# A two-layer decoder trunk on one core: branch B's units reordered, with scores two units ahead, and the sums for T1 to T4 read back from DRAM

## The chip, the cores and the metric

The kernel runs on one core of one Trainium2 chip. The metric is the device time of one execution in microseconds (us). The engines are named as in the profile: PE (TensorE, matmuls; PEld are its weight loads), DVE (VectorE), ACT (ScalarE), POOL (GpSimd) and SP (SyncE, which here only issues DMAs). L12 is line 12 of the kernel before.

## What is computed

Two layers, on x of 1024 tokens by 1024 channels, all in float32:

```python
h = rms_norm(x, g_pre)
p = h @ w_in          # 1024 x 7936: inputs of three branches, their gates, three merge gates
y_a = chunk_gmlp(u_a, v_a, ...) * silu(gate_a)            # per chunk of 128 tokens
y_b = sliding_window_attention(rope(q_b), rope(k_b), v_b, sinks) * silu(gate_b)
y_c = stick_breaking_attention(q_c, k_c, v_c) * silu(gate_c)
merged = sum(sigmoid(merge_gate_i + b_i) * (y_i @ w_branch_i) for i in "abc")
x = x + rms_norm(merged @ w_out, g_post)
```

Branch B has 8 query heads and 2 key heads of 64, in blocks of 128 queries that see 256 keys. Branch C has 4 heads of 128 and is causal over the whole sequence. Branch A normalises v_a per token and mixes the tokens of a chunk with a lower triangular matrix.

## The kernel before

**Precision.** PE multiplies in a format with fewer bits than float32. Every operand is therefore kept as two tiles, hi (a cast on ACT, L111) and lo (the rest, a subtraction on DVE, L112); `split` makes both. `mm3` (L127 to L130) adds up three matmuls: hi by hi, hi by lo, lo by hi. The transposed normalised input h stands in SBUF as such pairs, `h[hf]`, where hf is a half of 512 tokens.

**Tiles.** `new()` takes one of 27 slots of 128 x 1024 floats from the head of a queue, `done()` puts it back at the end. Which slot a tile gets, and so whose last reader it has to wait for, follows from the order of the program's text. PSUM has three kinds of buffers of two each: `pj`, `z` (1024 wide) and `ta`, which `ptr` (transposes) and `pav` (attention outputs) share.

**Order.** PE's order is the order of the text (`manual_schedule`). The order on ACT, DVE, POOL and SP is made by a planner at compile time from modelled durations; where two instructions are ready it takes the earlier one of the text, or the one under `high_priority`. At run time each engine and SP work strictly in that order, so an instruction that waits holds up all that follows on its engine. `tc.issue_after(ins)` puts the instructions of its block that run on the engine of `ins` behind `ins` in that engine's order.

**The stream.** The projections h @ w_in that the branches need are jobs in one queue (`queue_layer`). `proj_t` gives 16 tokens of three matmuls of 512 columns, `proj_n` 64 tokens of three of 256 columns. `fill(us)` runs tokens until their nominal values, 0.64 and 0.32, add up to us; `need(label)` runs tokens until a job is finished. `fill` puts PE work between the dependent steps of branches C and B while ACT, DVE and POOL prepare the next step. A job's weights are loaded and split when the job before it begins.

The order of jobs is: v0, q0, k0, q1, k1, v1, q2, k2, q3, k3 (branch C), kb, vb, qb0, ga0, ga1, qb1, qb2, qb3 (branch B and two gates of A), va0, va1, ua0 to ua3 (branch A).

When kb or a qb ends, `rope` (L278 to L292) rotates it: four DMAs on SP swap rows into a scratch tile, two products run on POOL (L289, L290), a sum on DVE (L291), then hi and lo on ACT and DVE (L303, L305 for keys; L342, L343 for queries).

**A layer's stages.** `first_h` (layer 0) or `project_out` of the layer before make h: `norm_a` squares, and scales a block of 128 tokens; `norm_b` transposes it on PE and splits it into h. Then come `branch_c`, `branch_b`, `dense`, `merges` and `project_out`.

- `branch_b` runs 8 units v, for a pair of heads hp = v // 2 and a half of the tokens. `scores(v)` makes 16 matmuls (L487), then evicts, masks and normalises on ACT, DVE and POOL. `transp` transposes the weights on PE (L520), splits them, and masks on POOL (L527). `attend` multiplies with v (L544) and evicts with ACT (L554) and DVE (L555). Here scores run one unit ahead. `FB` holds the fills: the first before the loop, then five per unit: before the attend of the unit before, before transp 0, before transp 1 (with `FB_MORE`), before attend(v,0), and after it.
- `Combine` prepares T1, T2, T4 and T3: sums and differences of quarters of h, right operands of a Strassen-like scheme with seven products. `total` (L679) adds hi and lo on POOL to get a quarter of h back. `go(spare)` takes as many of its six steps as there are slots free; it is called in units 6 and 7, and twice in `dense`.
- `dense` runs what is left of the stream, then 17 pairs of column blocks, each with the seven products B11, B21, T2, T3, T1, T4, B22 of 12 matmuls. Its pieces of branch A (`branch_a`, a generator, `next(a)`) begin with statistics and normalising of v_a on DVE (L614 to L620).
- `merges` multiplies gated branch outputs with w_branch, block by block; DVE gates the product (L930), POOL adds it (L935), and for the third branch a deferred `parts` splits the sum for `project_out`. A block half is 512 tokens of one `dm` (128 output channels): 12 matmuls.

Of the kernel before, what the change touches and what calls it, by code (L numbers as in the profile page):

```python
# [15 lines left out]
F32 = mybir.dt.float32  # L16
# [6 lines left out]
P = 128  # L23
# [12 lines left out]
FC = (0.6, 0.6, 1.2, 0.6)  # L36
FB = (4, 1.9, 1.9, 2.2, 2.8, 2.8)
FB_MORE = {1: 2.3, 2: 1.3}
# [3 lines left out]
def trunk(ctx, tc, x, w_in, gm_w_s, gm_b_s, gm_g, sinks, w_ba, w_bb, w_bc, b_merge, w_out,  # L42
# [187 lines left out]

    def norm_b(n, xn):

        hf, c = n // 4, (n % 4) * P
        pt = pz().rearrange("p (a b) -> p a b", a=KD)
        for k in range(KD):
            nc.tensor.transpose(pt[:, k], xn[:, k * P:(k + 1) * P], ident)
        split(h[hf][0][:, :, c:c + P], h[hf][1][:, :, c:c + P], pt)
        done(xn)


    def queue_layer(l, S):
# [111 lines left out]

        vcj(0); qk(0); qk(1); vcj(1); qk(2); qk(3)
        raw("kb", O_KB, 1.0, after_k)
        raw("vb", O_VB, 1.0, after_v)
        for hp in range(4):
            raw(("qb", hp), O_QB + hp * P, 0.125, lambda hp=hp: after_q(hp))
            if hp == 0:
                gate("a", 0)  # L360
                gate("a", 1)

        def ua(c):
# [4 lines left out]
            proj_t(f"ua{c}", l, O_UA + c * P, ev)  # L368
        va(0); va(1); ua(0); ua(1); ua(2); ua(3)

# [101 lines left out]
    def branch_b(l, S):  # L472
# [58 lines left out]
        def attend(v, q, p, o):  # L531
            hp, nh = divmod(v, 2)
            grp = hp // 2
            pc, pp, c, pv = p
            av = pav().rearrange("p (n e k) -> p n e k", n=2, e=2)

            def vs(nm, b):
                return S[nm][b // 4][:, ((b % 4) * 2 + grp) * P:((b % 4) * 2 + grp + 1) * P]
            for j in range(2):
                n = nh * 4 + q * 2 + j  # L540

                ops = [(vs("vd", n), t) for t in c] + ([(vs("dv", n), t) for t in pv] if n else [])
                for i, (w, t) in enumerate(ops):
                    nc.tensor.matmul(av[:, j], w, t.rearrange("p (e j) k -> p e j k", j=2)[:, :, j],  # L544
                                     start=i == 0, stop=i == len(ops) - 1)
            done(pc, pp)
            n = nh * 4 + q * 2
            tt = new()
            tmp = tt[:, :256].rearrange("p (n k) -> p n k", n=2)
            for e in range(2):  # L550

                a, b = slice(e * 64, e * 64 + 64), slice(64 - e * 64, 128 - e * 64)
                with tc.high_priority():
                    nc.scalar.copy(tmp[a], av[b, :, e])  # L554
                    nc.vector.tensor_tensor(o[a, n * P:(n + 2) * P].rearrange("p (n k) -> p n k", n=2), av[a, :, e],  # L555
                                            tmp[a], op=ALU.add)
            done(tt)
            if nh and q:
                nc.sync.dma_start(S["ob"][hp * P:(hp + 1) * P, :], o)
                done(o)  # L560

        need("ga0")
        fill(5)
        ready = {0: scores(0)}
        fill(FB[0])
        pend = None
        for v in range(8):
            if v % 2 == 0:
# [12 lines left out]
            fill(FB[2])  # L581
            s = ready.pop(v)
            p0 = transp(s, 0)
            fill(FB[3] + FB_MORE.get(v, 0))
            p1 = transp(s, 1)
            done(s)
            if v >= 6:
                S["T"].go(6)
            fill(FB[4])
            attend(v, 0, p0, o)  # L590
            fill(FB[5])
            pend = (v, 1, p1, o)
            if v == 7:
                S["T"].go(5)
        attend(*pend)
# [61 lines left out]
    class Combine:  # L657

        def __init__(self):
# [16 lines left out]
        def steps(self):  # L676
            def total(hf, k0, eng):
                r = new()
                eng.tensor_tensor(r.rearrange("p (k t) -> p k t", k=2), h[hf][0][:, k0:k0 + 2].bitcast(F32),  # L679
                                  h[hf][1][:, k0:k0 + 2].bitcast(F32), op=ALU.add)  # L680
                return r
# [5 lines left out]
            for kp in range(2):  # L687
                k0 = kp * 2
                r12, r11 = total(1, k0, nc.gpsimd), total(0, k0, nc.gpsimd)
                nc.vector.tensor_tensor(r11, r12, r11, op=ALU.subtract)  # L690
                keep("T1", r11)
                yield
                r22 = total(1, k0 + 4, nc.gpsimd)
                nc.vector.tensor_tensor(r12, r22, r12, op=ALU.subtract)
# [4 lines left out]
                yield  # L699
                r21 = total(0, k0 + 4, nc.gpsimd)  # L700
                nc.vector.tensor_tensor(r21, r21, r22, op=ALU.subtract)
# [15 lines left out]
    def dense(l, S):  # L717
# [165 lines left out]
    def merges(l, S):  # L883
# [25 lines left out]
        for i, (bi, br, dm) in enumerate(blocks):  # L909
# [11 lines left out]
            for hf in range(2):  # L921
# [4 lines left out]
                with tc.high_priority():  # L926
                    if bi == 0:
                        nc.vector.tensor_tensor(acc[dm][:, ts], sg[:, ts], z, op=ALU.mult)
                    else:
                        nc.vector.tensor_tensor(sg[:, ts], sg[:, ts], z, op=ALU.mult)  # L930
                if late:
                    late.pop()()
                if bi:
# [26 lines left out]
    def project_out(l, mg):  # L960
# [29 lines left out]
        for n in range(NB):  # L990
# [18 lines left out]
            if 2 <= n < 6:  # L1009
                norm_b(n - 2, xn.pop(n - 2))  # L1010
        for t in mg:
# [4 lines left out]
        done(gpre)  # L1016
        norm_b(4, xn.pop(4))
        tokens(2)
        norm_b(5, xn.pop(5))
        tokens(1)  # L1020
        norm_b(6, xn.pop(6))
        tokens(1)
        norm_b(7, xn.pop(7))
        tokens(4)
        return last

    def first_h():
# [11 lines left out]
        for n in range(NB + 2):  # L1039
            if n < NB:  # L1040
                xn[n], last = norm_a(xt[n], gpre)
            if 1 <= n <= NB:
                norm_b(n - 1, xn.pop(n - 1))
            if n >= 2:
                tokens(1)
# [23 lines left out]
    for l in range(L):  # L1069
        states.append({nm: dr.tile([512, T], F32, name=f"{nm}{l}") for nm in ("ga", "gb", "gc", "oa", "ob", "oc",  # L1070
                                                                                "ya", "yb", "yc")})
        states[l]["sg"] = dr.tile([3 * D, T], F32, name=f"sg{l}")

# [4 lines left out]
    with tc.manual_schedule(engines={mybir.EngineType.PE}):  # L1078
# [3 lines left out]
        for l in range(L):  # L1082
# [4 lines left out]
            need("k0")  # L1087
            S["T"] = Combine()
            branch_c(l, S)
# [43 lines left out]
```

## Time and profile before

| what | value |
|---|---|
| time, median of 3 runs | 2100.52 us (2100.18 to 2101.63) |
| time of the profiled execution | 2101.78 us |
| its span | 2100.1 us |
| mean granted clock of PE | 0.988 |
| DMA | 245.03 MB, mean 117 GB/s |

The profile's page gives the busy time of each engine within the span. Matmuls overlap, so PE's busy time contains no gaps between matmuls that follow each other, and its idle time is what waits leave. The granted clock is the share of full speed that PE was allowed; 1.00 is full. A row of waits reads "engine tile line <- who ended the wait: total us, times, longest". A row of a group reads "line engine operation out<-in shapes xcount | busy us, mean ns of one | idle before". A timeline row gives start and duration in us, and in brackets the idle time before it.

### The profile page before, as it was taken

The page shows a single profiled execution, that of the slowest core. Times are in us where ns is not written, and L with a number is a line of the kernel's source. Part 1 is how long each engine was busy: PE and PEld are TensorE (multiplying, and loading weights), DVE is VectorE, ACT ScalarE, POOL GpSimd, SP SyncE. Part 2 cuts the span into 40 slices and gives each one's busy share as a digit, 9 for nine tenths or more (in the row PEclk, how much of TensorE's full clock was granted, in tenths as well). Part 3 has the DMA queues.
Part 4 walks back from the last instruction along what each step waited for, and adds up shares of the span by engine and source line. Part 5 has one row for each costly group of instructions (what it writes and reads, how often), then busy time and mean ns, then how long its engine had stood idle before and what let it go on. Part 6 is the DMA issues. An engine that isn't in the chain of part 4 may idle for free. (4 is left out here: it accounts for less than half of the span.)

```text
span 2100.1 us, 26497 instructions
## 1 busy us (share of the span) xinstructions
PE 2015.5 (96%) x10193; PEld 1685.4 (80%) x10193; DVE 1222.6 (58%) x1601; ACT 801.4 (38%) x1471; POOL 539.1 (26%) x517
## 2 busy tenths in 40 slices
PE   8999897999999999999999998899899999999998
PEld 7898786977888888887898887689778888888876
DVE  5555644777676555644546566457667765555433
ACT  5444444543243334212334345444433443332121
POOL 0222313344333220240003122233533223103400
PEclk9999998999999999999999999999999999999999
DMA  4111222112766427632321111311147662376213
GB/s 161 34 47 32 70 71 65 37 50 81 266 235 231 140 87 264 221 110 81 111 71 31 49 53 41 91 51 51 41 141 253 237 220 94 120 254 216 81 50 130
DMA packets 148062, 245.03 MB, mean 117 GB/s; under 512 B 8104, under 2 KB 105440, under 8 KB 147936
## 3 DMA queue, kind: packets, MB, share of 16 engines
q1 hardware_dynamic: 141024, 218.17, 31.7%
q10 hardware_dynamic: 6912, 25.17, 3.0%
q8 instruction: 80, 1.31, 0.3%
q14 instruction: 46, 0.38, 0.1%
HBM read 166.76 MB, written 71.30 MB: 113 GB/s over the span
## 5 line engine op out<-in xcount | busy, mean ns | idle before, releaser
L128 PE MATMUL pj<-h,whi 128*128 128x512 f32 x700 | 286.3, 409 | 0.0
L129 PE MATMUL pj<-h,whi 128*128 128x512 f32 x700 | 278.3, 398 | 0.0
L130 PE MATMUL pj<-h,wlo 128*128 128x512 f32 x700 | 278.1, 397 | 0.0
L130 PEld LDWEIGHTS pj<-h,wlo 128*128 128x128 f32 x700 | 132.4, 189 | 31.8
L128 PEld LDWEIGHTS pj<-h,whi 128*128 128x128 f32 x700 | 133.2, 190 | 24.9
L129 PEld LDWEIGHTS pj<-h,whi 128*128 128x128 f32 x700 | 133.2, 190 | 23.5
L128 PE MATMUL pj<-whi,h 128*128 128x256 f32 x512 | 148.3, 290 | 0.0
L130 PE MATMUL pj<-whi,h 128*128 128x256 f32 x512 | 144.0, 281 | 0.9 <-DVE h L112 0.9
L129 PE MATMUL pj<-wlo,h 128*128 128x256 f32 x512 | 143.7, 281 | 0.0
L112 DVE TENSOR_TENSOR wlo<-wr,whi 128x1024 fp32r<-128x1024 f32 x80 | 104.9, 1314 | 65.4 <-ACT whi L111 65.4
L935 POOL TENSOR_TENSOR s<-s,s 128x512 f32<-128x512 f32 x56 | 78.6, 1407 | 240.5 <-DVE s L930 128.8
L111 ACT CAST whi<-wr 128x1024 fp32r<-128x1024 f32 x80 | 84.0, 1050 | 145.7 <-PE pj L129 94.4
L111 ACT CAST wop<-s 128x512 fp32r<-128x512 f32 x118 | 73.0, 620 | 171.1 <-PE pz L130 58.2
L112 DVE TENSOR_TENSOR wop<-wr,wop 128x512 fp32r<-128x512 f32 x120 | 103.6, 867 | 42.7 <-ACT wop L111 42.5
L111 ACT CAST wop<-wr 128x512 fp32r<-128x512 f32 x120 | 73.9, 619 | 140.3 <-PE ptr L130 31.3
L397 DVE TENSOR_TENSOR_SCAN s<-s,ones 128x128 f32<-128x128 f32 (+3 forms) x64 | 91.9, 1437 | 60.0 <-POOL s L392 59.7
L112 DVE TENSOR_TENSOR s<-ptr,s 128x512 fp32r<-128x512 f32 (+2 forms) x132 | 77.3, 589 | 67.3 <-ACT s L111 66.6
L112 DVE TENSOR_TENSOR wop<-s,wop 128x512 fp32r<-128x512 f32 x118 | 104.8, 888 | 18.2 <-ACT wop L111 17.9
L111 ACT CAST s<-s 128x512 fp32r<-128x512 f32 (+2 forms) x64 | 47.9, 751 | 171.2 <-POOL s L935 70.1
L128 PE MATMUL pj<-h,s 128*128 128x512 f32 x256 | 103.4, 404 | 5.8 <-ACT s L111 5.8
L130 PE MATMUL pj<-h,s 128*128 128x512 f32 x256 | 102.8, 402 | 1.8 <-DVE s L112 1.8
L129 PE MATMUL pj<-h,s 128*128 128x512 f32 x256 | 102.9, 402 | 0.0
(231 smaller groups left out, 5231.0 us busy)
## 6 DMA issues: line engine op xcount, KB each, us to landing
wr<-in_w_in_dram SPq DMA_DIRECT2D x96, 512.0 KB, 3.9
sg<-s ACTq DMA_DIRECT2D x48, 512.0 KB, 4.9
s<-sg SPq DMA_DIRECT2D x48, 512.0 KB, 5.5
s<-in_w_in_dram SPq DMA_DIRECT2D x28, 512.0 KB, 5.3
s<-in_x_dram SPq DMA_DIRECT2D x16, 512.0 KB, 4.4
wor<-in_w_out_dram SPq DMA_DIRECT2D x16, 512.0 KB, 3.6
s<-s SPq DMA_DIRECT2D x40, 128.0 KB, 2.3
oc<-s SPq DMA_DIRECT2D x8, 512.0 KB, 2.6
```

The lines of the kernel that those rows point to most:

```text
L111: nc.scalar.copy(hi, raw)
L112: nc.vector.tensor_tensor(lo, raw, hi.bitcast(F32), op=ALU.subtract)
L128: nc.tensor.matmul(acc, lh, rh, start=first, stop=False)
L129: nc.tensor.matmul(acc, lh, rl, start=False, stop=False)
L130: nc.tensor.matmul(acc, ll, rh, start=False, stop=last)
L397: nc.vector.tensor_tensor_scan(t1[:, :kl][:, ::-1], t1[:, :kl][:, ::-1], ones.to_broadcast([P, kl]), 1.0, op0=ALU.mult, op1=ALU.mult)
L935: eng.tensor_tensor(acc[dm][:, ts], acc[dm][:, ts], sg[:, ts], op=ALU.add)
```

## The change

- `queue_layer`: ga0 and ga1 go ahead of kb; va0 goes between qb1 and qb2, va1 behind qb3.
- `branch_b`: begins with `need(("qb", 1))` in place of `need("ga0")`, computes scores(0) and scores(1) ahead of the loop, and scores(v + 2) in unit v. The fills get shorter. cos, sin and the keys are given back in unit 5. `T.go` keeps 3 slots spare in place of 6 and 5. The eviction instructions of the last attend are remembered.
- `dense`: the first `next(a)` is put behind these instructions on ACT and DVE.
- `norm_b`: ACT also copies the transposed block to xn's slot, ahead of the split, and SP stores it to a DRAM tensor hT; `total` loads a quarter from hT by a DMA on SP in place of the sum on POOL.
- `merges`: the deferred split is put behind the gating instruction on DVE.

```diff
-FB = (4, 1.9, 1.9, 2.2, 2.8, 2.8)
+FB = (4, 1.5, 1.5, 1.8, 2.4, 2.4)
...
+        raw = xn
+        nc.scalar.copy(raw.rearrange("p (a b) -> p a b", a=KD), pt)
         split(h[hf][0][:, :, c:c + P], h[hf][1][:, :, c:c + P], pt)
-        done(xn)
+        nc.sync.dma_start(S["hT"].rearrange("(k p) t -> p k t", p=P)[:, :, n * P:(n + 1) * P],
+                          raw.rearrange("p (a b) -> p a b", a=KD))
+        done(raw)
...
-        vcj(0); qk(0); qk(1); vcj(1); qk(2); qk(3)
-        raw("kb", O_KB, 1.0, after_k)
-        raw("vb", O_VB, 1.0, after_v)
-        for hp in range(4):
-            raw(("qb", hp), O_QB + hp * P, 0.125, lambda hp=hp: after_q(hp))
-            if hp == 0:
-                gate("a", 0)
-                gate("a", 1)
...
-        va(0); va(1); ua(0); ua(1); ua(2); ua(3)
+        def qb(hp):
+            raw(("qb", hp), O_QB + hp * P, 0.125, lambda: after_q(hp))
+
+        vcj(0); qk(0); qk(1); vcj(1); qk(2); qk(3); gate("a", 0); gate("a", 1)
+        raw("kb", O_KB, 1.0, after_k)
+        raw("vb", O_VB, 1.0, after_v)
+        qb(0); qb(1); va(0); qb(2); qb(3); va(1); ua(0); ua(1); ua(2); ua(3)
...
-                    nc.scalar.copy(tmp[a], av[b, :, e])
-                    nc.vector.tensor_tensor(o[a, n * P:(n + 2) * P].rearrange("p (n k) -> p n k", n=2), av[a, :, e],
+                    S["b_act"] = nc.scalar.copy(tmp[a], av[b, :, e])
+                    S["b_dve"] = nc.vector.tensor_tensor(o[a, n * P:(n + 2) * P].rearrange("p (n k) -> p n k", n=2), av[a, :, e],
...
-        need("ga0")
-        fill(5)
+        need(("qb", 1))
+        fill(4)
         ready = {0: scores(0)}
+        fill(3)
+        ready[1] = scores(1)
         fill(FB[0])
...
-            if v + 1 < 8:
-                ready[v + 1] = scores(v + 1)
-            if v == 6:
+            if v + 2 < 8:
+                ready[v + 2] = scores(v + 2)
+            if v == 5:
                 done(S["cos"], S["sin"])
...
-                S["T"].go(6)
+                S["T"].go(3)
...
-            def total(hf, k0, eng):
+            def total(hf, k0):
                 r = new()
-                eng.tensor_tensor(r.rearrange("p (k t) -> p k t", k=2), h[hf][0][:, k0:k0 + 2].bitcast(F32),
-                                  h[hf][1][:, k0:k0 + 2].bitcast(F32), op=ALU.add)
+                nc.sync.dma_start(r.rearrange("p (k t) -> p k t", k=2), self.S["hT"].rearrange("(k p) t -> p k t", p=P)
+                                  [:, k0:k0 + 2, hf * HT:(hf + 1) * HT])
                 return r
...
-        next(a)
+        with tc.issue_after(S["b_act"].ins), tc.issue_after(S["b_dve"].ins):
+            next(a)
...
-                        nc.vector.tensor_tensor(sg[:, ts], sg[:, ts], z, op=ALU.mult)
+                        gated = nc.vector.tensor_tensor(sg[:, ts], sg[:, ts], z, op=ALU.mult)
                 if late:
-                    late.pop()()
+                    with tc.issue_after(gated.ins):
+                        late.pop()()
```

More of the change, by code (lines that the diff above doesn't have):

```diff
@@ L229, in norm_a, with norm_b @@
         return xn, last
-    def norm_b(n, xn):
+    def norm_b(S, n, xn):
         hf, c = n // 4, (n % 4) * P
@@ L692, in steps @@
                 yield
-                r22 = total(1, k0 + 4, nc.gpsimd)
+                r22 = total(1, k0 + 4)
                 nc.vector.tensor_tensor(r12, r22, r12, op=ALU.subtract)
@@ L1009, in project_out @@
             if 2 <= n < 6:
-                norm_b(n - 2, xn.pop(n - 2))
+                norm_b(states[l + 1], n - 2, xn.pop(n - 2))
         for t in mg:
@@ L1042, in first_h @@
             if 1 <= n <= NB:
-                norm_b(n - 1, xn.pop(n - 1))
+                norm_b(states[0], n - 1, xn.pop(n - 1))
             if n >= 2:
```

24 lines of the change are left out of this document (13 added, 11 removed).

## The prediction

> **What bounds the kernel now.** I read the page's head and part 1, then the waits of PE, then windows of 50 us and windows cut around each wait.
>
> ```profile
> span 2100.1 us, 26497 instructions
> PE 2015.5 (96%) x10193; PEld 1685.4 (80%) x10193; DVE 1222.6 (58%) x1601; ACT 801.4 (38%) x1471; POOL 539.1 (26%) x517
> 550.00:600.00 50.00, 50.00 (x216) 40.26 (x215) 41.23 (x48) 16.69 (x26) 12.04 (x10) 1.00 0.74 259
> ```
>
> The third line is a row by windows: from:to, length, busy us and count of PE, PEld, DVE, ACT and POOL, granted clock, DMA share, GB/s. PE is the bound, and the change leaves its 10193 matmuls as they are. A clean stretch runs 216 matmuls of 512 columns in 50 us, 0.2315 us each; a fill token of three of them (0.64 in the code) is 0.70 us. So only PE's idle time (84.6 us) and slow clock can move.
>
> ```profile
> PE pz L487 <- DVE s L343: 23.6, 4, 11.4
> PE pav L129 <- DVE s L112: 11.3, 16, 1.3
> PE ptr L520 <- DVE s L555: 9.8, 6, 2.8
> PE pz L128 <- ACT s L394: 7.3, 2, 3.7
> PE pj L128 <- ACT s L111: 5.8, 2, 3.0
> PE pav L544 <- POOL s L527: 2.0, 3, 1.2
> PE ptr L128 <- DVE s L815: 1.9, 1, 1.9
> PE pj L130 <- DVE s L112: 1.8, 2, 0.9
> PE pj L129 <- DVE s L112: 1.8, 1, 1.8
> PE ptr L129 <- DVE s L112: 1.8, 1, 1.8
> ```
>
> Columns: total us, times, longest. Nearly all come in pairs, one per layer.
>
> ```profile
> 327.60:334.50 6.90, 6.41 (x22) 5.62 (x23) 3.16 (x4) 1.23 (x3) 0.41 (x1) 0.51 0.01 2
> 249.10:252.50 3.40, 3.40 (x10) 2.52 (x9) 3.15 (x3) 2.47 (x3) 2.44 (x4) 0.50 0.00 0
> 457.30:460.70 3.40, 3.40 (x11) 2.81 (x11) 1.11 (x2) 1.17 (x2) 3.40 (x4) 0.50 0.00 0
> 966.60:972.70 6.10, 6.10 (x15) 4.75 (x16) 4.03 (x5) 2.46 (x5) 0.00 (x0) 0.50 0.54 178
> 2000.00:2050.00 50.00, 46.08 (x191) 36.46 (x190) 16.53 (x22) 11.47 (x24) 0.00 (x0) 0.97 0.16 53
> ```
>
> The first four windows lie just behind or around the four kinds of wait treated below: the granted clock is halved there, and half of such a stretch is lost on top of the wait.
>
> **What goes.** (a) End of branch C. kb's rope and casts sit among branch C's work (timeline of ACT: start, duration, engine, line):
>
> ```profile
> 245.12 2.11 ACT L303 CAST s<-s 64x1024 fp32r<-64x1024 f32 x2
> 247.13 0.80 ACT L394 ACTIVATE s<-pz 128x768 f32<-128x768 f32 x1
> ```
>
> The sigmoid L394, for which PE waits 3.65 us a layer (7.3 for two), stands behind kb's casts on ACT. In the new order ga0 and ga1 take that place, with one copy on ACT and one on DVE each and no rope, and kb ends only in the projections ahead of branch B, where PE waits for nothing on ACT but the eviction of its own banks. Gone: 3.65, the 1.3 just before it (the longest of the L129 <- L112 row), and 1.7 of clock (half of 3.4): 6.6 a layer. Other work will still bunch there; I leave 0.5 of it.
>
> (b) The wait of scores(2) for the rope of qb1: 11.8 a layer, and 3.4 of clock (half of 6.9): 15.2. After the change 4 + 3 + 4 us of fill and two units of scores lie between qb1's last matmul and scores(2), more than the 14 us that rope takes (below), and qb0 has all of qb1's projection and 4 us of fill.
>
> (c) Branch B's end. L520 waits 4.9 a layer for DVE's L555, which stands behind branch A's statistics and sums for T; L544 1.0; clock 1.7 once. POOL's sums also slow DVE:
>
> ```profile
> 471.11 5.21 POOL L679 TENSOR_TENSOR s<-h,h 128x1024 f32<-128x1024 f32 x2 [3.19 <-DVE s L555]
> 473.99 3.42 DVE L690 TENSOR_TENSOR s<-s,s 128x1024 f32<-128x1024 f32 x1
> 484.03 1.23 DVE L696 TENSOR_TENSOR s<-s,s 128x1024 f32<-128x1024 f32 x1
> ```
>
> The same subtraction takes 3.42 beside POOL and 1.23 alone. With the sums loaded by DMA, and the statistics ordered behind attend(7,1), both causes go: 9.8 + 2.0 + 1.7 = 13.5 for both layers.
>
> (d) The end of merges runs round a loop:
>
> ```profile
> 950.45 0.68 DVE L930 TENSOR_TENSOR s<-s,pz 128x512 f32<-128x512 f32 x1
> ...
> 952.58 0.62 ACT L111 CAST s<-s 128x512 fp32r<-128x512 f32 x1 [2.78 <-POOL s L935]
> 953.24 0.69 DVE L112 TENSOR_TENSOR s<-s,s 128x512 fp32r<-128x512 f32 x1 [2.11 <-ACT s L111]
> 953.85 0.68 DVE L930 TENSOR_TENSOR s<-s,pj 128x512 f32<-128x512 f32 x1
> ```
>
> From L930 to L930 it is 3.40 us, but PE needs 12 x 0.2315 = 2.8 for a block half, so DVE falls behind by 0.6 each and project_out starts late. Ordered behind the next L930, the split no longer stands in its way: each L930 waits for PE alone, and project_out's first reading of the last half comes 20 matmuls later. What is late then is nothing on PE's path. Gone: 3.8 a layer (L128 <- ACT, L130 <- DVE), and clock 3.0 and 1.5: 12.1. Sum of (a) to (d): 13.2 + 30.4 + 13.5 + 12.1 = 69.2.
>
> **What comes.** (e) qb2. va0 now runs ahead of it. Counting tokens: need(qb1) takes one of va0's 64; the fills up to FB[4] of v=0 take 60; FB[5] takes the last 3 and 3 of qb2; v=1 takes 3 + 3 + 7. That is qb2's sixteenth, just ahead of transp(1,1). Up to scores(4) PE has 4 transposes, 4 tokens, attend(1,0) with 8 matmuls of 256 columns, and 4 tokens: by starts rather than by the overlapping durations 0.4 + 2.8 + 1.0 + 2.8 = 7.0 us.
>
> ```profile
> L520 PE MATMUL ptr<-ident,s 128*128 128x128 f32 x128 | 19.7, 276 | 9.8 <-DVE s L555 9.8
> L544 PE MATMUL pav<-s,s 128*128 128x256 f32 x240 | 34.4, 282 | 2.0 <-POOL s L527 2.0
> ```
>
> (By these groups, busy time over count, 0.6 and 1.15: 7.4.) What rope takes shows at qb1:
>
> ```profile
> 314.33 0.60 ACT L275 ACTIVATE s<-pj 128x512 f32<-128x512 f32 x1
> ...
> 319.30 2.34 POOL L289 TENSOR_TENSOR s<-s,s 128x1024 f32<-128x1024 f32 x1 [8.70 <-DMA s<-s]
> ...
> 327.64 0.80 PE L487 MATMUL pz<-s,s 128*128 128x256 f32 x2 [11.38 <-DVE s L343]
> ```
>
> 13.3 us from L275 to PE's start, 14.0 with the wait ahead of L275. So scores(4) waits 7.0, and 0.5 for the second head: 7.5. Below: nothing, if rope took 7; above: 10, if DVE and ACT are busy. Behind scores(4) everything on PE waits. Clock: between 1.7 and 3.4, I take 2.6. Cost 10.1 a layer, 20.2. The Trainium skill ("TensorE: Matmul & The Clock Gate", Part 1, "What's actually happening") says the gate halves after an idle window of some 3.4 us on a free-running grid. The trace agrees (3.4 at 0.50); by that rule alone the least clock cost is 1.7, and the sum 1.8 us lower.
>
> (f) With two units of scores held, I count only 1 to 5 slots free from v=1 to v=4. attend(2,0)'s scratch tile gets qb3's slot, which rope still reads. ACT's copy of that attend then waits, and with it what ACT has queued behind (casts of weights, the eviction of scores(5)), while PE has some 10 us of fill ahead of transp(3,0), which needs the bank. The shorter fills, 3 tokens (2.1 us) a unit fewer, also leave less ahead of each transp. No row has this; I take 2.0 a layer, from 0 to 5: 4.0.
>
> (g) Start of dense. Before, 15 of ua3's 16 tokens (10.5 us) lay between attend(7,1) and the first product; by the same count 2 do now (1.4). In dense's go(0), the load for the second T2 gets the slot of branch B's o, so it waits for the store of ob, on SP; behind it queue the load for T4 and pair 1's weights (needed 20 us later).
>
> ```profile
> ob<-s SPq DMA_DIRECT2D x8, 512.0 KB, 3.0
> wr<-in_w_in_dram SPq DMA_DIRECT2D x96, 512.0 KB, 3.9
> s<-sg SPq DMA_DIRECT2D x48, 512.0 KB, 5.5
> L555 DVE TENSOR_TENSOR s<-pav,s 64x256 f32<-64x256 f32 x64 | 26.8, 419 | 20.5 <-ACT s L554 19.7
> L614 DVE BATCH_NORM_STATS2 st<-s 128x6 f32<-128x512 f32 x16 | 10.4, 680 | 0.1
> L620 DVE TENSOR_SCALAR s<-s,mv,rs 128x512 f32<-128x512 f32 x16 | 8.1, 539 | 0.1
> ```
>
> From attend(7,1)'s end: eviction 2.4 (two times a copy on ACT and L555's 0.42, with the waits between), store 3.0, load 4.0 (a load from hT isn't in the trace; nearest are wr in a quiet stretch, which I take, and sg in a busy one, 5.5), two subtractions of 1.23, cast 1.0, split 1.2 and 0.3 of waits: 14.4. PE wants the low part of T2's second half after 1.4 and 31 matmuls of the products, 8.6. Wait 5.8; with some of the statistics (18.5/2 = 9.3 us a layer, now here) between, 6.5, and clock 2.0: 8.5 a layer, bounds 0 and 13. The waits there before (1.8, 1.8, 1.9) go: net 17 - 5.5 = 11.5. The Trainium skill ("DMA: Bandwidth & Descriptors", "Anatomy of one DMA") prices a DMA of POOL's path at 2.0 us fixed and the rest at 436 GB/s, and calls the fixed part longest where the target is HBM. By that the two DMAs would be 6.4 us (an estimate) in place of 7.0, the sum 1.2 lower, and the store the slower of the two; the rows have it the other way, 3.0 against 3.9.
>
> (h) norm_b's copy stands on ACT ahead of the cast of h.
>
> ```profile
> 10.40:26.20 15.80, 14.70 (x103) 14.31 (x104) 14.98 (x19) 15.57 (x27) 0.41 (x2) 1.00 0.75 258
> L111 ACT CAST h<-pz 128x1024 fp32r<-128x1024 f32 x16 | 16.2, 1015 | 6.8 <-PE pz L236 6.7
> ```
>
> The fourth number is ACT: 15.57 of 15.8 us while four blocks pass, so the copies add up to 4 x 1.0 us, less what little PE has in hand; I take 3.3, from 0 to 4. Between the layers the eight blocks are spread over project_out, and no wait of PE falls there: nothing, as long as ACT keeps that idle time. The 16 stores of hT wait on SP for the copy; behind them stand rows of x and weights that are wanted a block later, and DMA has room (0.75 at its busiest).
>
> Sum: 69.2 - 20.2 - 4.0 - 11.5 - 3.3 - 1.0 = 29.2. The profiled execution took 2101.78 (span 2100.1 and 1.7 around it), 1.3 above the median: 2100.5 - 29.2 = **2071**.
>
> **Rivals.**
> - The load of T2 stays hidden (another slot, or an early o): the start of dense costs what it did, 2060. Against it: the slot order. 15%.
> - qb2's rope stays hidden: 20 less, 2051; with the former too, 2039. Against it: 14.0 against 7.0 us. 12%.
> - The orderings don't bite: the planner keeps the splits ahead of L930 (12.1 more, 2083) or statistics in branch B's end (9.8 more, 2093). For it: the planner sets all but PE's order; against it: an edge is explicit. 12%.
> - Slower: the start of dense becomes the bound. Five loads share the DMA engines (2.6 MB at the 259 GB/s of the first window quoted is 10.1 us, not 4.0: 6.1 more), and all 9.3 us of statistics stand ahead of T2's subtractions: 15.4 more a layer, 2102; with (f) at 5 too, 2108. It decides from 14.6 us more a layer. For it: nothing on DVE is ordered there but by the planner. 7%.
> - Slot waits in branch B worse than 5 a layer: 2080 to 2098. 8%.
>
> **Numbers.** My forecast (2062 to 2082) has 46%. A measurement here tells about 0.2% (4.2 us) from no change. The slower rival gives 0.06 of slower and 0.01 of same, the last one 0.02 of same: faster 0.91, same 0.03, slower 0.06. The range, 2046 to 2093, leaves out both hidden chains and the worst of the last two.
>
> **What would show it.** Right: no wait of L487 at scores(2), but 6 to 10 us at scores(4), v=2; no wait behind L394 near 248; L930 every 2.8 us; a wait of 4 to 9 us in T2's product for DVE's split, with the ob store and a load from hT just ahead; first_h 3 us longer. Wrong: the PE wait gone at scores(4), T loads landing before attend(7,1), or DVE's L930 still every 3.4 us.

## The result, and the profile after

| | before | after |
|---|---|---|
| median of 4 runs | 2100.62 us (2100.18 to 2101.63) | 2087.85 us (2087.08 to 2088.75) |
| span of the profiled execution | 2100.1 us | 2086.1 us |
| PE idle (span less busy) | 84.6 us | 71.1 us |

The ratio is 0.9934, with an interval from 0.9922 to 0.9946: the kernel is 13 us faster, where 29 were forecast. Lines below are those of the kernel after; the scores are now L488, transp L521, attend L545 to L556, the rope L279 to L295 and L346, L347, the hT load L683, the T subtractions L694, L698, L700, L705, and the merges' gating L935. In the other runs the same instruction can stand a few lines off.

Part 1 of the page of after:

```profile
PE 2015.0 (97%) x10193; PEld 1689.0 (81%) x10193; DVE 1218.3 (58%) x1601; ACT 815.9 (39%) x1485; POOL 496.5 (24%) x501
```

PE's matmuls are the same 10193. The waits of PE in after (total us, times, longest):

```profile
PE pz L488 <- DVE s L347: 16.2, 4, 7.7
...
PE pz L488 <- DVE s L501: 7.8, 2, 3.9
PE pj L128 <- ACT s L111: 7.4, 1, 7.4
PE ptr L128 <- ACT s L111: 6.4, 1, 6.4
...
PE ptr L521 <- DVE s L556: 3.2, 2, 1.6
...
PE pj L129 <- DVE s L112: 1.5, 1, 1.5
PE ptr L129 <- DVE s L112: 1.5, 1, 1.5
PE pav L545 <- POOL s L528: 1.2, 2, 0.6
```

Against the list of before: the waits behind branch C's sigmoid and in the merges are gone, and of those of branch B's end only the 1.2 of L545 is left. The 3.2 of L521 stand elsewhere, at 396 us and its place in layer 2, where attend(2,0)'s copy on ACT waits for qb3's rope (start, duration, idle time before):

```profile
396.13 0.37 ACT L555 COPY s<-pav 64x256 f32<-64x256 f32 x1 [0.93 <-DVE s L347]
```

Four other kinds are new, each once a layer. L488 <- L347 looks like the old row L487 <- L343, but it stands at another place: at 360 us, scores(4) waiting for qb2's rope, not scores(2) for qb1's. L488 <- L501 is new and nobody's rope: scores(2) waits 3.9 us for a bank that scores(1) has not been read out of. The two L128 <- L111 and the two L129 <- L112 (1.5) are the start of dense, where T2's high and then low part are late. Windows cut where the granted clock was half, behind scores(2), scores(4) and the start of dense (from:to, length, busy time of PE, PEld, DVE, ACT, POOL, clock, DMA share, GB/s):

```profile
322.40:329.20 6.80, 6.15 (x29) 6.15 (x30) 4.70 (x8) 2.98 (x13) 0.41 (x1) 0.50 0.00 1
363.30:373.60 10.30, 5.03 (x19) 4.55 (x20) 4.34 (x5) 3.80 (x6) 1.04 (x2) 0.50 0.00 0
482.80:493.00 10.20, 5.56 (x14) 4.17 (x15) 10.02 (x15) 5.31 (x6) 0.00 (x0) 0.50 0.00 0
```

Half of PE's busy time in such a window is lost on top of the wait: 3.1, 2.5 and 2.8 us in layer 1 (3.0, 2.4 and 3.2 in layer 2).

**The wait that was not foreseen.** ACT around scores(1) and scores(2) of layer 1 (start, duration, and in brackets the idle time before):

```profile
313.94 1.28 ACT L509 ACT_TABLE_LOAD   x1 [4.14 <-DVE mx L506]
...
316.41 2.10 ACT L346 CAST s<-s 64x1024 fp32r<-64x1024 f32 x2
...
320.57 1.04 ACT L500 COPY s<-pz 128x512 f32<-128x512 f32 x2
```

The exps of scores(0), L509, have ACT; they wait 4.14 us for the maximum on DVE, and qb1's casts L346 stand among them. PE computed scores(1) from 312.5 to 314.6, but the copies that free its banks come behind the last exp, at 320.57, and DVE's part of it, behind the normalising of scores(0) (L513), still later:

```profile
312.31 1.55 DVE L506 SCALAR_TENSOR_TENSOR mx<-mx,nsnk 128x8 f32<-128x8 f32 x1
...
322.28 1.32 DVE L501 COPY_PREDICATED s<-mprev,pz 128x512 f32<-128x512 int32 x2
```

There are two z buffers and a unit of scores needs both, so scores(2), ready at 319.1, stands until 323.05: 3.91 us, then 6.8 us at half clock. In both layers that is 7.8 + 6.1 = 13.9 us.

**The start of dense.** SP in layer 1, the waits of SP's queue from 474 to 478 us, then DVE and ACT:

```profile
472.38 0.33 SPq L560 DMA_DIRECT2D ob<-s  x1
...
474.36 0.37 SPq L780 DMA_DIRECT2D wr<-in_w_in_dram  x1
476.69 0.37 SPq L683 DMA_DIRECT2D s<-hT  x1
```

```profile
SPq L683 <- DMA ob<-s: 1.9, 1, 1.9
```

```profile
481.11 1.27 DVE L617 BATCH_NORM_STATS2 st<-s 128x6 f32<-128x512 f32 x2
482.30 1.20 DVE L698 TENSOR_TENSOR s<-s,s 128x1024 f32<-128x1024 f32 x1
...
483.59 1.18 DVE L700 TENSOR_TENSOR s<-s,s 128x1024 f32<-128x1024 f32 x1
...
485.83 1.21 DVE L705 TENSOR_TENSOR s<-s,s 128x1024 f32<-128x1024 f32 x1
486.97 1.21 DVE L112 TENSOR_TENSOR s<-s,s 128x1024 fp32r<-128x1024 f32 x1
```

```profile
484.81 1.05 ACT L111 CAST s<-s 128x1024 fp32r<-128x1024 f32 x1 [0.22 <-DVE s L700]
```

The load waited for the ob store, and was issued 4.3 us after it (4.1 in layer 2). The load of weights ahead of it on SP, issued at 474.36, was not what held it. From its landing near 481.4 to T2's low part at 488.2 it took 6.8 us. Two pieces of DVE's work lengthen that: the statistics L617 run until 482.4, after the landing, and T4's subtraction L705 goes ahead of T2's low part, whose high part is ready at 485.9. T3's split cost nothing here: ACT was idle for 0.22 us before T2's cast, for T2's subtraction L700.

**The merges.** DVE's gating in after:

```profile
936.23 0.69 DVE L935 TENSOR_TENSOR s<-s,pz 128x512 f32<-128x512 f32 x1 [1.51 <-PE pz L130]
```

It waits 1.51 us for PE and comes every 2.80 us (the next at 939.03), where it was 3.40 and PE waited for it.

### The profile page after: what moved, and what is told of

It reads as the page before. It is cut to its first block, busy times and chain, and to the rows that moved or that the text cites. A ratio compares the mean times of both kernels' runs of the same rounds, so it can differ in the third digit from the quotient of the medians.

```text
span 2086.1 us, 26587 instructions
## 1 busy us (share of the span) xinstructions
PE 2015.0 (97%) x10193; PEld 1689.0 (81%) x10193; DVE 1218.3 (58%) x1601; ACT 815.9 (39%) x1485; POOL 496.5 (24%) x501
## 4 chain that ended last, share of the span: by engine, by line
PE 87%; DVE 4%; issue 3%; ACT 2%; POOL 2%; DMA 1%; SPq 0%; POOLq 0%; DVEq 0%; ACTq 0%
PE pj L129 16%; PE pj L128 16%; PE pj L130 16%; PE pz L129 5%; PE pz L130 5%; PE pz L128 5%; PE ptr L129 5%; PE ptr L130 5%; PE ptr L128 5%; PE pz L488 2%; PE ptr L415 1%; PE pav L129 1%; PE pav L545 1%; PE pav L130 1%; POOL s L396 1%
## 5 line engine op out<-in xcount | busy, mean ns | idle before, releaser
L128 PE MATMUL pj<-h,whi 128*128 128x512 f32 x700 | 285.3, 408 | 0.0
L129 PE MATMUL pj<-h,whi 128*128 128x512 f32 x700 | 277.3, 396 | 0.0
L128 PEld LDWEIGHTS pj<-h,whi 128*128 128x128 f32 x700 | 132.3, 189 | 24.4
L112 DVE TENSOR_TENSOR wlo<-wr,whi 128x1024 fp32r<-128x1024 f32 x80 | 107.0, 1341 | 75.9 <-ACT whi L111 75.5
L129 PEld LDWEIGHTS pj<-h,whi 128*128 128x128 f32 x700 | 132.2, 189 | 22.9
L128 PE MATMUL pj<-whi,h 128*128 128x256 f32 x512 | 149.0, 291 | 1.0 <-ACT h L111 1.0
L111 ACT CAST whi<-wr 128x1024 fp32r<-128x1024 f32 x80 | 84.1, 1051 | 163.0 <-PE pj L129 109.3
L129 PE MATMUL pj<-wlo,h 128*128 128x256 f32 x512 | 144.8, 283 | 0.0
L111 ACT CAST wop<-s 128x512 fp32r<-128x512 f32 x118 | 73.2, 620 | 183.0 <-PE pz L130 60.7
L111 ACT CAST wop<-wr 128x512 fp32r<-128x512 f32 x120 | 74.4, 620 | 154.2 <-PE ptr L130 38.7
L398 DVE TENSOR_TENSOR_SCAN s<-s,ones 128x128 f32<-128x128 f32 (+3 forms) x64 | 87.7, 1370 | 63.7 <-POOL s L393 63.7
L112 DVE TENSOR_TENSOR wop<-wr,wop 128x512 fp32r<-128x512 f32 x120 | 99.8, 836 | 31.9 <-ACT wop L111 31.3
L112 DVE TENSOR_TENSOR wop<-s,wop 128x512 fp32r<-128x512 f32 x118 | 107.3, 909 | 16.3 <-ACT wop L111 16.0
L112 DVE TENSOR_TENSOR s<-ptr,s 128x512 fp32r<-128x512 f32 (+2 forms) x132 | 77.3, 589 | 64.9 <-ACT s L111 64.4
L129 PE MATMUL pj<-h,s 128*128 128x512 f32 x256 | 102.0, 398 | 0.0
L128 PE MATMUL pj<-h,s 128*128 128x512 f32 x256 | 101.2, 395 | 0.0
L130 PE MATMUL pj<-h,s 128*128 128x512 f32 x256 | 100.6, 393 | 0.0
L130 PEld LDWEIGHTS pj<-whi,h 128*128 128x128 f32 x512 | 98.0, 191 | 2.6 <-DVE h L112 2.6
```

Of the source, the lines that this page charges most:

```text
L111: nc.scalar.copy(hi, raw)
L112: nc.vector.tensor_tensor(lo, raw, hi.bitcast(F32), op=ALU.subtract)
L128: nc.tensor.matmul(acc, lh, rh, start=first, stop=False)
L129: nc.tensor.matmul(acc, lh, rl, start=False, stop=False)
L130: nc.tensor.matmul(acc, ll, rh, start=False, stop=last)
L398: nc.vector.tensor_tensor_scan(t1[:, :kl][:, ::-1], t1[:, :kl][:, ::-1], ones.to_broadcast([P, kl]), 1.0, op0=ALU.mult, op1=ALU.mult)
```

## The experiments

My theory after the traces: most parts of the change do what they say, but **two units ahead** creates two waits in branch B (scores(2) for scores(1)'s bank, scores(4) for qb2's rope), and with the shorter rest of the stream one at the start of dense; together these give back everything but the merges' gain. The rival: the loads from hT and norm_b's copies, or slots, cost it.

**One part alone.** The merges' order put into the kernel before:

```diff
                 if late:
-                    late.pop()()
+                    with tc.issue_after(gated.ins):
+                        late.pop()()
```

> The kernel before with one part of the change alone: the deferred split of merges behind the gating instruction on DVE. Theory: this part is worth the whole of its term, 3.8 us of waits a layer and 3.0 and 1.5 us of half clock, about 12: 2088 to 2089, which is also about all that the whole change gains. L930 then comes every 2.8 us. Rival: part of what the changed kernel gains there comes from its other edits (the lag of DVE at the start of merges), so that this alone gives less than 8: above 2092.

2088.8 us (2087.45 to 2089.63), ratio 0.9943 [0.9929, 0.9958]. The merges' waits are gone and the rest is that of before, as this row of the waits of PE shows:

```profile
PE pz L487 <- DVE s L343: 23.6, 4, 11.4
```

So this one edit is worth 12 us and makes up the whole net gain. All other edits of the change together come to about nothing: what they take away they bring back.

**One unit ahead in the kernel after.** The keys, cos and sin are given back in unit 6 again; everything else stays:

```diff
         fill(3)
-        ready[1] = scores(1)
         fill(FB[0])
...
-            if v + 2 < 8:
-                ready[v + 2] = scores(v + 2)
-            if v == 5:
+            if v + 1 < 8:
+                ready[v + 1] = scores(v + 1)
+            if v == 6:
```

> The changed kernel with scores one unit ahead again (cos, sin and keys given back in unit 6 as before), the rest as changed. Theory: the two new waits of branch B come of the lead of two alone. The wait for the eviction of scores(1)'s bank (3.9 us and 3.1 of half clock a layer) goes as one unit's evictions no longer meet another's exponentials, and scores(4) comes a unit of 16 us later, so that qb2's rope is done: 7.7 + 0.5 and 2.5 of half clock a layer go too. 2088 - 14 - 21 = 2053. Rival 1: without the lead, transposes wait for the softmax of their unit (L513), and the gain is given back: 2070 to 2088, with waits of L521 for DVE's L513. Rival 2: slots, not the lead, set these waits: no change.

2059.95 us (2058.26 to 2060.43), ratio 0.9804 [0.9788, 0.982]. No row of L488 is left among the waits of PE; the longest two behind first_h are those of dense, 8.2 and 7.4:

```profile
PE pj L128 <- ACT s L111: 8.2, 1, 8.2
...
PE ptr L521 <- DVE s L556: 6.2, 4, 1.9
```

The second unit of lead, the heart of the change, costs 28 us. The theory had 7 us more: the waits of dense became longer by 0.8 and 0.9 us, L521's went from 3.2 to 6.2, and one of them is followed by half clock in each layer, 1.7 us.

**The bank of scores(1).** In the kernel after, only the 3 us of fill between the first two units are moved:

```diff
         ready = {0: scores(0)}
-        fill(3)
         ready[1] = scores(1)
+        fill(3)
         fill(FB[0])
```

> The kernel after, with the 3 us of fill that stand between scores(0) and scores(1) moved behind scores(1); scores(0) where it was. Theory (the 3.91 us wait at scores(2) is that of scores(1)'s copy on ACT, which comes up only after the exps of scores(0) have been taken: when both units' copies come ahead of the exps, the bank is free 6 us sooner): scores(2)'s wait and its clock loss go, 13.9 us, and scores(1) waits 1 to 2 us at each half of it for scores(0)'s copies, 2 to 4 a layer: 2078, 2074 to 2082. Rival (the exps go first all the same, or the two units' copies queue up behind qb1's casts): the wait moves to scores(1) in full, 2084 to 2092.

2077.21 us (2076.48 to 2077.71), ratio 0.9887 [0.9872, 0.9902]: 10.6 us less than after. ACT in layer 1 of this run:

```profile
311.54 0.59 ACT L500 COPY s<-pz 128x512 f32<-128x512 f32 x1 [0.89 <-PE pz L488]
312.75 0.59 ACT L500 COPY s<-pz 128x512 f32<-128x512 f32 x1 [0.62 <-PE pz L488]
314.82 1.28 ACT L509 ACT_TABLE_LOAD   x1 [1.48 <-DVE mx L506]
```

The copies of scores(1), 311.54 and 312.75, now stand ahead of the exps, right behind that of scores(0), and the row L488 <- L501 is gone. From scores(0) to scores(2) PE has as much fill as in after, and the exps begin no sooner. What changed is that scores(1)'s copies come 8 us earlier because they no longer stand behind those exps.

The other way to give scores(1) time, 4 us of fill moved from ahead of scores(0) to behind scores(1):

```diff
         need(("qb", 1))
-        fill(4)
...
-FB = (4, 1.5, 1.5, 1.8, 2.4, 2.4)
+FB = (8, 1.5, 1.5, 1.8, 2.4, 2.4)
```

> The kernel after, with the 4 us of fill ahead of scores(0) moved behind scores(1) (no fill before scores(0), 8 in place of 4 before scores(2)); every product and its count as before. Theory (the 3.91 us wait at scores(2), with the 6.8 us at half clock that follows it, comes from ACT, where the copy that frees scores(1)'s bank stands behind the exps of scores(0); with 4 us more between scores(1) and scores(2) it is done in time): the two waits of 3.91 and their clock loss of 3.0 a layer go, 13.9 in all: 2074, 2072 to 2078. Rival (what holds the exps is qb1's rope and casts, which do not move, so that the exps end no sooner): a wait of 3 to 4 us stays at scores(2), 2084 to 2089.

2096.01 us (2093.61 to 2097.28), ratio 0.9975 [0.9966, 0.9984]. Neither came: the wait at scores(2) went as in the theory, but the time is 8 us worse than after, mainly because one row of PE's waits has grown:

```profile
PE pz L488 <- DVE s L347: 25.3, 8, 8.4
```

Eight waits in place of four: scores(0), at 304 us, now waits 3.2 and 0.7 us for qb0's rope, which those 4 us had hidden. Neither side had thought of it. The two waits of dense grew too, by 0.4 us in layer 1 and by 2.4 in layer 2.

**qb2 sooner.**

```diff
-        qb(0); qb(1); va(0); qb(2); qb(3); va(1); ua(0); ...
+        qb(0); qb(1); qb(2); va(0); qb(3); va(1); ua(0); ...
```

> The changed kernel with qb2 ahead of va0 in the stream, the rest as changed. Theory: the wait at scores(4) (8.1 us and 2.5 of half clock a layer) is the 14 us of rope against 7 us of PE work behind qb2; with va0 behind qb2 it goes: 2088 - 21 = 2067. qb3 still ends 10 us of fill ahead of scores(6). Rival: the tiles of qb2 held longer take slots, and waits for slots in units 1 to 4 give back 5 us a layer or more: above 2075.

2073.69 us (2073.05 to 2074.3), ratio 0.9872 [0.9857, 0.9887]. scores(4)'s wait is gone, as it must be if it was qb2's rope. 14 of its 21 us are gained; the remainder comes back in attends that wait for POOL, at scores(2) (8.8 for 7.8) and in dense (7.9 for 7.4 in layer 1, 7.8 for 6.4 in layer 2):

```profile
PE pj L128 <- ACT s L111: 7.9, 1, 7.9
...
PE pav L545 <- POOL s L528: 3.9, 4, 2.2
```

**The quarters summed on POOL again**, without hT, its copies and its stores:

```diff
-                nc.sync.dma_start(r.rearrange(...), self.S["hT"].rearrange(...)[:, k0:k0 + 2, hf * HT:(hf + 1) * HT])
+                nc.gpsimd.tensor_tensor(r.rearrange(...), h[hf][0][:, k0:k0 + 2].bitcast(F32),
+                                        h[hf][1][:, k0:k0 + 2].bitcast(F32), op=ALU.add)
```

> The changed kernel with T1 to T4's quarters made by sums on POOL again, and without hT, its copies and stores; order, lead and fills as changed. Theory: the long wait at the start of dense (8.9 and 8.0 us, 2.8 and 3.2 of half clock) is the load of T2's quarter behind the store of ob; POOL's sum takes 2.4 where store, load and issue take 9. It shrinks by about 4 us a layer, first_h gives 2.4 back, and POOL beside DVE costs 1 to 3 a layer in branch B's end: 2079 to 2084. Rival: the wait is there because only 2 tokens are left of the stream, whatever makes the quarters: 2086 to 2092, with the wait still 7 us or more.

2098.74 us (2096.36 to 2102.45), ratio 0.9993 [0.9984, 1.0003]: 11 us worse than after, beyond both. The rival that blames the loads from hT falls, as far as the whole kernel goes: sums in their place cost more. At the start of dense the picture is mixed. In layer 1 the wait for T2's high part is shorter, 4.2 for 7.4, but one of 3.4 for branch B's last eviction comes ahead of it; in layer 2 it is 9.9 for 6.4, without any load. And branch B's end is worse:

```profile
PE ptr L128 <- ACT s L111: 9.9, 1, 9.9
...
PE ptr L517 <- DVE s L552: 4.8, 4, 1.6
PE pav L541 <- POOL s L524: 4.6, 5, 1.2
```

**The order at the start of dense.** T2 subtracted and split first, T3's and T4's work behind T2's low part:

```diff
...
-                nc.vector.tensor_tensor(r12, r22, r12, op=ALU.subtract)
-                self.r3.append(r12)
-                nc.vector.tensor_tensor(r22, r22, r11, op=ALU.subtract)
-                keep("T2", r22)
-                done(r11)
+                nc.vector.tensor_tensor(r11, r22, r11, op=ALU.subtract)
+                with tc.high_priority():
+                    keep("T2", r11)
+                with tc.issue_after(self.lo.ins):
+                    nc.vector.tensor_tensor(r12, r22, r12, op=ALU.subtract)
+                self.r3.append(r12)
...
```

> The kernel after, with T2's second quarter subtracted and split ahead of T3's subtraction, T3's placing and T4's subtraction (T2 written over T1's scratch tile, the others issued after T2's lo). Theory (of the start of dense, the part from the landing of the load to T2's lo, 482.3 to 488.2 us in the trace of after, holds 2.3 us of other work: T3's subtraction of 1.20 and cast of 1.05 ahead of T2's hi, T4's subtraction of 1.21 ahead of T2's lo): 1.8 to 2.3 a layer, 2083 to 2084.5. Rival (the load's landing alone sets it, and T3's product, the next one, waits instead): 2086.5 to 2088.5.

2090.23 us (2089.44 to 2091.3), ratio 0.995 [0.9935, 0.9965]: no gain, 2.4 us worse. In the waits of PE (L689 is T2's cast here, L828 the copy of B11's product):

```profile
PE ptr L128 <- ACT s L689: 8.1, 1, 8.1
...
PE pj L128 <- ACT s L689: 6.6, 1, 6.6
...
PE ptr L128 <- ACT s L828: 3.0, 1, 3.0
```

In layer 1 the wait for T2's high part is 0.8 us shorter, and a later product takes back more, 3.0. In layer 2 it is 1.7 longer. The slot of T1's scratch tile is also held longer, so other waits move, and this run does not isolate the order: what that alone costs stays open. As a cure it failed.

It shows one thing more. The slots fall otherwise here, so that all loads from hT are issued ahead of the ob store, and still T2's subtraction L699 begins only at 485.00. SP and DVE in layer 1:

```profile
467.73 5.12 SPq L683 DMA_DIRECT2D s<-hT  x4
478.28 0.33 SPq L560 DMA_DIRECT2D ob<-s  x1
```

```profile
485.00 1.21 DVE L699 TENSOR_TENSOR s<-s,s 128x1024 f32<-128x1024 f32 x1
```

On DVE, T1's subtraction and split and a part of the statistics come first, and on ACT T2's cast then stands behind a cast of weights that waits for its load. So the ob store alone does not set the wait of dense: with it out of the way, the queues of DVE and ACT held T2 nearly as long.

**The order of the statistics dropped:**

```diff
-        with tc.issue_after(S["b_act"].ins), tc.issue_after(S["b_dve"].ins):
-            next(a)
+        next(a)
```

> The kernel after, without the order that holds branch A's statistics behind branch B's last eviction (the two lines around the first next(a) dropped). Theory (that order is what took away the 9 us of branch B's end): L556 waits behind the statistics L617 again, at each half 2 to 4 us, 2092 to 2097. Rival (it was the T sums' absence from POOL, beside which DVE ran slower, so that the order is worth little, and statistics done sooner leave DVE free at the start of dense): 2084 to 2089.

2092.09 us (2091.45 to 2096.97), ratio 0.9964 [0.9952, 0.9977]. The order is worth 4 us, but at neither place expected: branch B's end stays as it was, and T2's low part is later, 3.7 in place of 1.5 us in each layer:

```profile
PE pj L129 <- DVE s L112: 3.7, 1, 3.7
```

With the order dropped, branch B's end stays relieved; with the order kept and the sums on POOL (the run of that kind above) it is not. So it was the sums.

**The gates put back behind qb0:**

```diff
-        ... qk(3); gate("a", 0); gate("a", 1)
+        ... qk(3)
...
-        qb(0); qb(1); va(0); ...
+        qb(0); gate("a", 0); gate("a", 1); qb(1); va(0); ...
```

> The kernel after, with gate a0 and gate a1 put back behind qb0, so that kb, vb and qb0 come ahead of them again; nothing else. Theory (the move of the gates is what took kb's rope and casts off the last units of branch C, 16.1 us by the traces): branch C's last units wait for DVE and ACT again, 6 to 7 us a layer with 1.6 of clock: 2103, 2099 to 2106. Rival (with the merges' and branch B's changes kb's rope would be hidden anyway, or the gates between qb0 and qb1 give back as much at scores(2), since qb0's casts are then long done): 2086 to 2094.

2104.28 us (2101.41 to 2106.04), ratio 1.0014 [1.0005, 1.0023], 16.4 us more than after. Branch C's wait is back, with the number it had before:

```profile
PE pz L128 <- ACT s L395: 7.3, 2, 3.7
```

**More of the stream for dense.** Two tries on the kernel with one unit ahead. The first drops the 4 us ahead of scores(0), and has T2 first and norm_b's copy behind the split:

```diff
         need(("qb", 1))
-        fill(4)
...
-        nc.scalar.copy(raw.rearrange("p (a b) -> p a b", a=KD), pt)
         split(h[hf][0][:, :, c:c + P], h[hf][1][:, :, c:c + P], pt)
+        nc.scalar.copy(raw.rearrange("p (a b) -> p a b", a=KD), pt)
```

> The kernel after with scores one unit ahead again, as in the run of that kind (2060), and three more edits: no fill ahead of scores(0), so that 4 us more of the layer's stream are left for the start of dense; T2 first, as in the run beside it; norm_b copies the transposed block for hT behind the split in place of ahead of it. Theory: the 8.18 and 7.38 us waits at T2 shrink by 4.2 for the longer stream and by 2 for T2's order, with 1.7 of clock a layer, and first_h is 2.4 shorter: 2060 - 8.4 - 4 - 3.4 - 2.4 = 2042, 2038 to 2048. Rival (scores(0) 4 us sooner runs into qb0's and qb1's ropes, and the unit's evictions take back what the start of dense gains): above 2052.

2072.25 us (2070.43 to 2073.52), ratio 0.9864 [0.9849, 0.9878]: 12 us worse than 2060. T2's high part is now waited for by 0.3 and 1.6 us only, in place of 8.2 and 7.4, so a longer stream does cover most of that. But scores(0) waits for qb0's rope again, attends wait for POOL, and with T2 early the product behind it waits (L826, the copy of B11's product):

```profile
PE pav L545 <- POOL s L528: 10.7, 9, 2.8
...
PE pz L488 <- DVE s L347: 7.8, 4, 3.2
...
PE ptr L128 <- ACT s L826: 5.8, 1, 5.8
```

The second takes the fill from units 1 and 2 instead, leaves T2's order alone, and keeps the copy behind the split:

```diff
-FB_MORE = {1: 2.3, 2: 1.3}
+FB_MORE = {}
```

> The kernel after with scores one unit ahead (2060 in the earlier run), the 2.3 and 1.3 us of extra fill in units 1 and 2 dropped, so that they are left for the start of dense, and norm_b's copy for hT behind its split. Theory: the wait at T2 in each layer is shorter by the tokens kept, 4 us, with 1 of clock, and first_h by 2 to 2.4: 2060 - 8 - 2 - 2.2 = 2048, 2045 to 2052. Rival (units 1 and 2 need that fill: their attends and transp wait for the exps and for POOL's copies of the halves): 2054 to 2064.

**2035.82 us** (2034.25 to 2039.68), ratio 0.9696 [0.968, 0.9713]: the best here, 52 us under after and below what the theory gave. The page's first part, and SP at the end of branch B in layer 1:

```profile
PE 1997.9 (98%) x10193; PEld 1675.8 (82%) x10193; DVE 1211.6 (60%) x1601; ACT 813.7 (40%) x1485; POOL 499.8 (25%) x501
```

```profile
447.19 1.10 SPq L682 DMA_DIRECT2D s<-hT  x1
...
450.39 0.33 SPq L560 DMA_DIRECT2D ob<-s  x1
```

The last load from hT is issued 3.2 us ahead of the ob store, where it came 4.3 us behind it in after. So it cannot be waiting for that store's slot, and PE no longer waits for T2. The program's text gives the reason, when `new()` and `done()` are followed through it. With more tokens left a ua tile takes its slot later, so at the start of unit 7 `go` finds one more step's worth of slots free; the load of T2's second quarter then gets a slot of attend(7,1)'s weights, where in after and in the 2060 kernel it gets the one that o gives back. This would explain why 3.6 us of fill (2.3 and 1.3) took away some 9 us of waiting a layer; it was not tried apart from the longer stream. What that fill had hidden came up in part: transposes wait 4.7 us for the normalising of their scores (L521 <- DVE L513), where the 2060 kernel had 0.2. The place of norm_b's copy has its share too: what lies ahead of branch B is 2 to 4 us shorter than in after and in the 2060 kernel. PE's idle time is 34.6 us of a span of 2032.5, and its busy time 17 us less than in after for the same matmuls, as the clock is seldom halved now.

**The same with the sums on POOL**, without hT:

> The kernel of the run at 2035.8 (scores one ahead, without the extra fill of units 1 and 2), with T1 to T4 from sums on POOL again and no transposed input in DRAM (so norm_b's copy and store fall away too). Theory (with 6 us more of the stream at its end the start of dense is covered either way, so that the copy in DRAM is worth nothing in this kernel; norm_b's copies gone are worth 1 to 2 us at the start): 2033 to 2038. Rival (as with two units ahead, where the sums on POOL cost 11 us: they stand in POOL's queue with the masks of branch B, and the last of them still comes too late): 2042 to 2052.

2063.08 us (2061.73 to 2064.28), ratio 0.9821 [0.9804, 0.9837]: 27 us worse, beyond the rival too. POOL and DVE in unit 6 of layer 1, and the wait of PE:

```profile
413.76 8.09 POOL L678 TENSOR_TENSOR s<-h,h 128x1024 f32<-128x1024 f32 x3
```

```profile
416.19 3.41 DVE L689 TENSOR_TENSOR s<-s,s 128x1024 f32<-128x1024 f32 x1 [2.57 <-POOL s L678]
```

```profile
PE ptr L517 <- DVE s L552: 11.5, 3, 5.7
```

Three sums run back to back, DVE's subtraction beside them takes 3.41 us where others take 1.2, and PE's transposes wait 5.7 us for an eviction that stands behind DVE's subtractions. The transposed input in DRAM, with its copies and stores, is thus worth 27 us here; in the kernel after it was worth 11.

## Why the prediction was wrong

It had the right sign and the time within its range, but the gain was 13 us where 29 were given. By steps, for both layers, waits and half clock together (the measured ones from the traces of before and after):

| step | predicted | measured |
|---|---|---|
| (a) branch C's end, less the 1.0 left in C | -12.2 | -15.8 |
| (b) scores(2)'s wait | -30.4 | -29.0, and **+13.9** new |
| (c), (f) branch B's end, slot waits | -9.5 | -9.1 |
| (d) merges | -12.1 | -12.2 |
| (e) scores(4) for qb2's rope | +20.2 | +21.1 |
| (g) start of dense | +11.5 | +17.4 |
| (h) first_h | +3.3 | +2.4 |
| sum | -29.2 | -11.3 |

The figure of (h) is the shift of what follows first_h; the others are waits and half clock. The span fell by 14.0; the 2.7 us between that and the sum lie in short gaps that I have not put down to a step.

- **(b) is the step that failed.** "After the change 4 + 3 + 4 us of fill and two units of scores lie between qb1's last matmul and scores(2), more than the 14 us that rope takes": that was true, and the rope's wait went in full. But the step asked only about the wait that it removed. scores(2) also needs both banks of scores(1), and these are emptied by instructions that stand on ACT and DVE behind the exps and the normalising of scores(0). The trace of after shows the queue, and moving one fill (2077.2) takes that wait away while all else stays. The risk could have been read from the kernel: two buffers, a unit that fills both, and a program text in which scores(0)'s exps come ahead of scores(1)'s copies. Which of them goes first is the planner's choice, though: the text has the same order in the 2077.2 run, where the copies went first.
- **(g) was right in kind, and too small by 5.9.** The wait of T2's load for the ob store is in the trace. The chain from attend(7,1)'s end to T2's low part, taken as 14.4 us, took 18.1 in layer 1: the load followed the store by 4.3 us and landed 4.7 later, where 3.0 and 4.0 were assumed, and behind the landing 6.8 us passed in place of 5.0, with statistics and T4's subtraction ahead of T2's work on DVE. It was also no fixed price: in the 2035.8 kernel it is absent. And the store is not its only cause, as the run with T2 first shows.
- (e) was right: the count of tokens gave 7.5 us a layer, and the two waits together are 8.1; sooner projection of qb2 removed it.
- (d) was right to 0.1, and shown alone (2088.8).
- (a) was right in its cause (2104.3 with the gates put back) and low by 3.6: beside the two waits that I counted there were two of 0.6, one of 0.5 and one of 1.3 in the same stretch, and of the 1.0 that I left only 0.4 stayed.
- (c) was a little high, 13.5 for 12.3, and wrong in one of its two causes: of the sums on POOL and the order of the statistics, it was the sums.
- (f) was right in place and cause, and near in size: attend(2,0)'s copy waits for qb3's rope, as the row of 396.13 shows, and PE's next transposes wait 1.6 us a layer, 3.2 for the 4.0 given.
- (h) was a little high: 2.4 for 3.3.
- Of the rivals, none was this one. "Slot waits in branch B worse" gave a time near the result (2080 to 2098) for another reason; I count that as chance.

What the forecast could have had: with 13.9 in (b) and the dense start as measured, its own sum is 29.2 - 13.9 - 5.9 = 9.4, 2091, some 3 us from the measured 2087.85.

## What to carry to other kernels

When work is moved one step further ahead, ask what its result is written into and who empties that, in queue order: with two buffers a second unit of lead needs the first unit's read-out to stand ahead of the previous unit's long chain, or the lead turns into a wait. Take a bundle of edits apart before judging it: here one edit in the merges was the whole net gain, the second unit of lead cost 28 us, and the costly-looking DRAM copy was worth 27 us once the rest was in order. Filler work is a budget: move it from where little waits (units 1 and 2) to where a chain starts late (dense), and look at what each fill hides before taking it away, as the 4 us ahead of scores(0) did.

## What the runs showed of the hardware

A wait of the same length did not cost the same clock. In the run with T2 first, scores(2) waits the same 3.91 us as in after, but here only the first of two windows of 3.4 us behind it is at half clock, where in after it is 6.8 us:

```profile
323.00:326.40 3.40, 2.94 (x13) 2.94 (x14) 2.39 (x4) 0.65 (x2) 0.38 (x1) 0.50 0.00 0
326.40:329.80 3.40, 3.40 (x30) 3.40 (x30) 2.59 (x6) 2.83 (x14) 0.03 (x1) 1.00 0.01 2
```

So the same wait lost 1.5 us there and 3.1 in after. The Trainium skill ("TensorE: Matmul & The Clock Gate", Part 1, "What's actually happening") lets the clock come back only after a busy window of some 3.4 us; that fits here. The wait of this run ends at 323.46, 0.5 us into a window that begins at 323.0, and that of after 0.65 us into one that begins at 322.4. PE was busy for 2.94 us of the first of these windows and for 2.75 of the second, and only behind the first did the clock come back. No threshold follows from that: elsewhere in this same run (490.26 to 493.68) a window with 2.78 us was enough, and in before (327.60 to 331.00) one with 2.90 was not. Sums of waits can be off by this much a place without any step being wrong, and differences of 2 or 3 us between these runs should not be read closely.
